# Modulation matmuls four in a row on one 1024-column tile, with loads two groups ahead, in a two-layer decoder step

## The chip, the cores and the metric

The kernel runs on one core of a Trainium2 chip, as one program. The time is the device time of one execution, in microseconds (us), the median of several runs. The engines are PE (TensorE, matmuls; its weight loads are listed apart as PEld), DVE (VectorE), ACT (ScalarE), POOL (GpSimd) and SP (SyncE), whose queue issues the transfers between HBM and the on-chip memory. Each engine, SP too, takes its instructions in one fixed order, and an instruction that waits holds up all that stand behind it on the same engine.

## The reference, cut to what matters

512 prompt tokens and 8 x 4 sample tokens (544 columns in all, in two halves of 272) go through two layers. Each layer has a mixer and a convolutional FFN, and both are wrapped in RMS norms with a shift, a scale and a gate per sequence (nine sequences: the prompt and eight samples), which come out of the conditioning vector c:

```python
c_act = jax.nn.silu(c)
for l in range(DEPTH):
    mod = (c_act @ w["ada_w"][l] + w["ada_b"][l])[:, None, :]      # (sequences, 1, 6 * 1024)
    sh1, sc1, g1, sh2, sc2, g2 = jnp.split(mod, 6, axis=-1)
    h = _rmsnorm(x, ng[0]) * (1 + sc1) + sh1
    y = mixer(h)                                                   # layer 0: _mixer_ab, layer 1: _mixer_cd
    x = x + g1 * _rmsnorm(y, ng[1])
    h = _rmsnorm(x, ng[2]) * (1 + sc2) + sh2
    y, f_new = _conv_ffn(h, f_prev, w["ffn_w_up"][l], ...)
    x = x + g2 * _rmsnorm(y, ng[3])
```

The matrix `ada_w` is 1024 x 6144 per layer in fp32, 50 MB in both, and is needed for nine rows only.

## The kernel before, in words

**The GEMMs.** The large products run in `gemm` and `mm` (lines 522 to 563). A fp32 weight block of 1024 x 128 comes in two raw tiles of 128 x 512 (256 KB each). `load_w` (504 to 512) issues the load on SP, lets ACT write a high part `whi` (line 510) and DVE or POOL the rest `wlo` (line 511). The input is kept likewise as `Hhi` and `Hlo`. Each of the eight 128-row pieces of a block then takes three products (lines 527, 529, 531) on two halves of 272 columns, 48 matmuls per block. The first blocks of a GEMM (its lead) and the last (its tail) are worked half by half. The raw tiles rotate through a ring of seven places with the tag `wraw` in the pool `wp`; `whi` and `wlo` have rings of eight. A tile takes the next place of its ring in the order in which the code asks for it, and may be written once the last reader of what was there is done.

**The modulation.** `ada(l, s)` (397 to 430) makes a third of one layer's modulation: 2048 columns, six calls in all. Per step k of eight it loads four tiles of 128 x 512 (line 403) and multiplies each with the 32 columns of `cact` (line 404), one in each of the four 32-column groups of PE, into one PSUM tile `psada`. After step 8 ACT copies `psada` to `adaev` (line 407, a tile of the norm pool), four PE transposes turn it (`psadat`, line 410), and DVE adds the bias and makes the scales cA and the gates cG (lines 411 to 429). The tiles come from the ring `wraw` in the start, later from a pool of six, then of four.

**The order.** `weave` (316) runs a GEMM block by block and a second generator beside it: after each block that takes one step, so the modulation of the next stage is spread over the GEMM of this one. `delay`, `pace` and `slow` (325 to 341) set how many steps per block. A scheduler then sets each engine's order from the whole program, so a matmul of the modulation stands where its load is expected, also in the middle of a block. The stages are: the start (modulation of layer 0's first third, X, the norm's `psn` sums, lines 440 to 449), mixer 0 with `w_abi` and `w_abo` from about 47 to 245 us, a junction (`postres` and `premod`, lines 461 to 502), FFN 0 with `w_up0` and `w_dn0` to about 660 us, mixer 1, FFN 1.

**Bias vectors.** `bias_vectors` (1188 to 1201), woven into FFN 0 ahead of layer 1's modulation, makes the attention bias in three steps. Each loads `ohp`, multiplies (`psrv`, line 1198), copies on ACT (line 1199) and stores to `rvd` in HBM through SP (line 1200). Its tiles come from the same pool as the modulation's.

Of the kernel before, what the change touches and what calls it, by code (L numbers as in the profile page):

```python
# [41 lines left out]
XRB = 6  # L42
# [225 lines left out]
def build(nc, tc, ctx, t):  # L268
# [120 lines left out]
    apool = []  # L389

    def ada_tile():
        if apool:
            ap, n = apool[-1]
            return ap.tile([P, CH, HT], F32, name="adaw", bufs=n).rearrange("p a n -> p (a n)")[:, 0:512]
        return wp.tile([P, 512], F32, name="adaw", tag="wraw", bufs=WRAW)

    def ada(l, s):
        ps = psum1("psada")
        for k in range(KB):
            for j in range(4):  # L400
                wt = ada_tile()
# [15 lines left out]

        def ng(i):
            oo = PAR["norm_g"][0] + (l * 4 + i) * KB
            return par[:, oo:oo + KB].unsqueeze(2).to_broadcast([P, KB, NMOD])  # L420

        mb = mods[l]
        if s == 0:
            V.scalar_tensor_tensor(cA[l][0], mb[:, 8:16, :], 1.0, ng(0), op0=ADD, op1=M)
        elif s == 1:
            V.tensor_tensor(cG[l][0], mb[:, 16:24, :], ng(1), op=M)
        else:
            V.scalar_tensor_tensor(cA[l][1], mb[:, 32:40, :], 1.0, ng(2), op0=ADD, op1=M)
# [93 lines left out]
    def mm(ps, wt, src, h0, h1):  # L522
        last = len(wt) - 1
        for i, (whi, wlo) in enumerate(wt):
# [93 lines left out]
    def ffn(l, nxt, side, pre):  # L618
# [55 lines left out]
        def body():  # L674
# [613 lines left out]
```

## Time and profile before

| | us |
|---|---|
| median of 3 runs | 1501.05 (1498.82 to 1502.52) |
| profiled execution, its own time | 1496.03 |
| its span, first to last instruction | 1494.3 |
| PE busy in the span | 1417.8 (95%) |
| modulation matmuls (line 404), busy | 102.6 |
| mean granted PE clock | 0.978 of full |

The profile is one execution; busy time counts each microsecond of an engine once. Matmuls overlap, so that a start-to-start distance tells more of their cost than a duration. A row of the timeline gives the start, the length up to the end of the last of the instructions that it groups, and in brackets the idle time before it and what ended that. An fp32 matmul leaves two records.

### The profile page before, as it was taken

To read this page: it belongs to the slowest core of one execution; us is meant where nothing else is said; L and a number is where in the kernel's file an instruction comes from. 1 tells how busy PE (TensorE), PEld (TensorE's weight loads), DVE (VectorE), ACT (ScalarE), POOL (GpSimd) and SP (SyncE) were. 2 spreads that over 40 slices of the span, in tenths; PEclk is the share of its full clock that TensorE was granted. 3 is DMA by queue.
4 is the path that set the end of the run, shared out by engine and by line. 5 is a ranking of instruction groups with operands and counts; after the bars stand their busy time and mean duration, and the time that the engine had idled before them with its cause. 6 is when DMAs were issued, how large, how long until landed. Compare 5 with 4: busy or idle time off the path is not lost.

```text
span 1494.3 us, 26853 instructions
## 1 busy us (share of the span) xinstructions
PE 1417.8 (95%) x10354; PEld 1271.0 (85%) x10354; DVE 882.1 (59%) x1788; ACT 618.8 (41%) x1145; POOL 170.6 (11%) x384
## 2 busy tenths in 40 slices
PE   6899997999999999999799999999699999999995
PEld 2578897988798798899699999678599999999995
DVE  1664427753165346446859979652886456456457
ACT  2322235743244234235652442643674444244244
POOL 0210014110011001001500000000521011011011
PEclk9799998999999999999999999999899999999998
DMA  7775633325445546544236245446122332332311
GB/s 264 242 253 187 201 106 100 103 98 180 160 155 194 161 139 212 165 158 186 89 113 197 94 141 178 135 146 239 57 85 69 103 93 71 104 91 65 113 51 61
DMA packets 112633, 207.72 MB, mean 139 GB/s; under 512 B 20884, under 2 KB 33684, under 8 KB 111992
## 3 DMA queue, kind: packets, MB, share of 16 engines
q1 hardware_dynamic: 112504, 206.00, 42.5%
q8 instruction: 81, 1.33, 0.4%
q14 instruction: 48, 0.39, 0.1%
HBM read 198.63 MB, written 34.39 MB: 156 GB/s over the span
## 4 chain that ended last, share of the span: by engine, by line
PE 88%; DVE 6%; DMA 2%; ACT 2%; issue 1%; SPq 0%; POOL 0%; POOLq 0%; DVEq 0%; ACTq 0%
PE psmm L527 23%; PE psmm L531 23%; PE psmm L529 23%; PE psada L404 6%; PE psn L442 2%; PE psmh L529 2%; PE psmh L527 2%; PE psmh L531 2%; PE pso L1013 1%; PE psl L979 1%; PE psl L981 1%; DVE X L492 1%; DVE Yf L491 1%; DVE Y L491 1%; DVE Hlo L481 1%
## 5 line engine op out<-in xcount | busy, mean ns | idle before, releaser
L510 ACT ACTIVATE whi<-wraw 128x512 fp32r<-128x512 f32 (+1 forms) x404 | 239.8, 600 | 511.4 <-PE psmm L529 411.6
L527 PE MATMUL psmm<-Hhi,whi 128*128 128x272 f32 x2028 | 435.9, 291 | 1.0 <-DVE extu L750 1.0
L531 PE MATMUL psmm<-Hhi,wlo 128*128 128x272 f32 x2028 | 431.4, 289 | 0.3 <-POOL wlo L511 0.3
L529 PE MATMUL psmm<-Hlo,whi 128*128 128x272 f32 x2028 | 430.0, 288 | 0.0
L511 DVE TENSOR_TENSOR wlo<-wraw,whi 128x512 fp32r<-128x512 f32 (+1 forms) x374 | 240.8, 649 | 303.4 <-ACT whi L510 288.3
L527 PEld LDWEIGHTS psmm<-Hhi,whi 128*128 128x128 f32 x2028 | 321.4, 189 | 24.3 <-issue 12.6
L529 PEld LDWEIGHTS psmm<-Hlo,whi 128*128 128x128 f32 x2028 | 322.5, 189 | 9.0 <-issue 9.0
L531 PEld LDWEIGHTS psmm<-Hhi,wlo 128*128 128x128 f32 x2028 | 321.5, 189 | 9.9 <-issue 9.2
L527 PE MATMUL psmm<-act_hi,whi 128*128 128x272 f32 x624 | 135.5, 290 | 0.0
L531 PE MATMUL psmm<-act_hi,wlo 128*128 128x272 f32 x624 | 135.3, 289 | 0.0
L529 PE MATMUL psmm<-act_lo,whi 128*128 128x272 f32 x624 | 132.7, 288 | 0.0
L578 DVE SCALAR_TENSOR_TENSOR fz<-fext,par,fz 128x560 f32<-128x560 f32 x88 | 70.5, 801 | 74.3 <-ACT fz L577 74.2
L404 PE MATMUL psada<-adaw,cact 128*32 128x512 f32 x384 | 102.6, 628 | 8.3 <-DMA adaw<-ada_w 8.3
L527 PEld LDWEIGHTS psmm<-act_hi,whi 128*128 128x128 f32 x624 | 99.6, 188 | 11.8 <-issue 8.4
L531 PEld LDWEIGHTS psmm<-act_hi,wlo 128*128 128x128 f32 x624 | 99.6, 188 | 7.6 <-issue 7.5
L529 PEld LDWEIGHTS psmm<-act_lo,whi 128*128 128x128 f32 x624 | 99.1, 188 | 0.8 <-issue 0.8
L577 ACT ACTIVATE fz<-fext,par 128x560 f32<-128x560 f32 x88 | 75.2, 855 | 34.5 <-DVE fext L647 34.5
L874 DVE SCALAR_TENSOR_TENSOR zd<-extd,par,zd 128x512 f32<-128x512 f32 x120 | 87.0, 746 | 0.7
L569 POOL COPY fso<-fext 128x2 f32<-128x2 f32 x88 | 23.1, 263 | 530.6 <-ACT fext L646 530.6
L579 DVE SCALAR_TENSOR_TENSOR fz<-fext,par,fz 128x560 f32<-128x560 f32 x88 | 70.5, 801 | 2.7
L646 ACT ACTIVATE fext<-psmm 128x512 f32<-128x512 f32 (+1 forms) x88 | 49.7, 564 | 51.1 <-PE psmm L531 51.1
L527 PE MATMUL psmh<-Hhi,whi 128*128 128x272 f32 x148 | 48.2, 326 | 16.1 <-ACT Hhi L479 14.5
(260 smaller groups left out, 1692.9 us busy)
## 6 DMA issues: line engine op xcount, KB each, us to landing
adaw<-ada_w SPq DMA_DIRECT2D x192, 256.0 KB, 3.6
wraw<-w_up SPq DMA_DIRECT2D x176, 256.0 KB, 3.0
wraw<-w_dn SPq DMA_DIRECT2D x64, 256.0 KB, 2.8
o_c<-cache SPq DMA_DIRECT2D x8, 2040.0 KB, 10.0
wraw<-w_cdi SPq DMA_DIRECT2D x52, 256.0 KB, 4.6
wraw<-w_abi SPq DMA_DIRECT2D x32, 256.0 KB, 4.5
o_c<-cache SPq DMA_DIRECT2D x8, 1016.0 KB, 7.1
kc<-kc SPq DMA_DIRECT2D x28, 256.0 KB, 3.7
```

The lines of the kernel that those rows point to most:

```text
L404: PE.matmul(ps[32 * j:32 * j + 32, :], cact[:, k, :], wt, start=(k == 0), stop=(k == KB - 1))
L442: PE.matmul(ps, ones, a, start=(i == 0), stop=(i == n - 1))
L510: A.activation(hi[:, :n], raw[:, :n], AF.Copy)
L511: eng.tensor_tensor(lo[:, :n], raw[:, :n], hi[:, :n], op=SUB)
L527: PE.matmul(ps[:, h, :HT], whi, xhi[:, h, :], start=(i == 0), stop=False)
L529: PE.matmul(ps[:, h, :HT], whi, xlo[:, h, :], start=False, stop=False)
L531: PE.matmul(ps[:, h, :HT], wlo, xhi[:, h, :], start=False, stop=(i == last))
L577: A.activation(z[:, :n], ext[:, 2:2 + n], AF.Identity, bias=b, scale=w[:, 2:3])
L578: V.scalar_tensor_tensor(z[:, :n], ext[:, 1:1 + n], w[:, 1:2], z[:, :n], op0=M, op1=ADD)
L579: V.scalar_tensor_tensor(z[:, :n], ext[:, 0:n], w[:, 0:1], z[:, :n], op0=M, op1=ADD)
L646: A.activation(fpr(ext, 2, h0, h1), cpr(ps, h0, h1), AF.Copy)
L874: V.scalar_tensor_tensor(cpr(z), ip, dw[:, i:i + 1], cpr(z), op0=M, op1=ADD)
```

## The change

`ada` takes a list of halves of the old calls. A step k of a half has four matmuls of 256 columns (line 420 of the changed code) that read one tile of 128 x 2 x 512, loaded by one transfer of 512 KB (line 409). Three such tiles rotate in a pool of their own, first the one of the start, later one of mixer 0 or of FFN 0. Loads are asked for two steps ahead of the matmuls. `tc.issue_after` holds each group of four behind the last matmul of the newest GEMM block, which `mm` notes in `newest`. As soon as step 8 of a half is asked for, `ada_out` does what follows it: `adaev`, now 128 x 256, comes from the weights' ring `wraw`; two matmuls with a selector `ssel` replace the four transposes and write only the 36 columns that are used; DVE does half of each sum. The tiles of `bias_vectors` (`bv`) come from the ring `wraw` too. In the start the statistics of both halves are made early (`xstat`), `xprep` and `first` of the second half move behind the first half of `w_abi`'s lead, and the normalised tiles `xr` come from the norm pool. The pacing is set anew for each stage.

```diff
-XRB = 6
+ADB = (3, 3)
...
+    ssel = cp.tile([P, 4, NMOD], F32, name="ssel")
+    apool = [st0]
+    newest = []
     def ada_tile():
-        if apool:
-            ap, n = apool[-1]
-            return ap.tile([P, CH, HT], F32, name="adaw", bufs=n).rearrange("p a n -> p (a n)")[:, 0:512]
-        return wp.tile([P, 512], F32, name="adaw", tag="wraw", bufs=WRAW)
-    def ada(l, s):
-        ps = psum1("psada")
-        for k in range(KB):
-            for j in range(4):
-                wt = ada_tile()
-                o = s * 2048 + j * 512
-                SY.dma_start(wt, t["ada_w"][l, k, :, o:o + 512])
-                PE.matmul(ps[32 * j:32 * j + 32, :], cact[:, k, :], wt, start=(k == 0), stop=(k == KB - 1))
-            yield
-        ev = np_.tile([P, 512], F32, name="adaev", tag="nsq", bufs=NSQ)
+        return apool[-1].tile([P, 2, 512], F32, name="adaw", bufs=ADB[len(apool) - 1])
+    def ada(halves, per, ahead):
+        todo = [(l, s, q, k) for l, s, q in halves for k in range(KB)]
+        tiles = []
+        def load():
+            if todo[len(tiles):]:
+                l, s, q, k = todo[len(tiles)]
+                tiles.append(ada_tile())
+                SY.dma_start(tiles[-1], t["ada_w"][l].rearrange("k p (s a q n) -> s q k p a n", s=3, a=2, q=2)[s, q, k])
+        for _ in range(ahead):
+            load()
+        for i, (l, s, q, k) in enumerate(todo):
+            load()
+            if k == 0:
+                ps = psum1("psada")[:, 0:256]
+            wt = tiles[i]
+            with tc.issue_after(newest[0]) if newest else nullcontext():
+                for j in range(4):
+                    PE.matmul(ps[32 * j:32 * j + 32, :], cact[:, k, :], wt[:, j // 2, 256 * (j % 2):256 * (j % 2) + 256],
+                              start=(k == 0), stop=(k == KB - 1))
+            if k == KB - 1:
+                ada_out(l, s, q, ps)
+            if i % per == per - 1:
+                yield
+    def ada_out(l, s, q, ps):
+        if q == 0 and l == 0 and s == 0:
+            V.tensor_copy(ssel, ident.rearrange("p (j n) -> p j n", j=4)[:, :, 0:NMOD])
+        ev = wp.tile([P, 256], F32, name="adaev", tag="wraw", bufs=WRAW)
         A.activation(ev, ps, AF.Copy)
-        pt = psum1("psadat")
-        for c in range(4):
-            PE.transpose(pt[:, c * P:(c + 1) * P], ev[:, c * P:(c + 1) * P], ident)
+        pt = psum1("psadat")[:, 0:8 * NMOD].rearrange("p (j c n) -> p j c n", j=4, c=2)
+        for c in range(2):
+            PE.matmul(pt[:, :, c, :], ev[:, c * P:c * P + P], ssel, start=True, stop=True)
+        mb = mods[l][:, s * 16:s * 16 + 16, :].rearrange("p (a q c) n -> q p a c n", a=2, q=2)[q]
         o = PAR["ada_b"][0] + l * 48 + s * 16
-        V.tensor_tensor(
-            mods[l][:, s * 16:s * 16 + 16, :].rearrange("p (j c) n -> p j c n", c=4),
-            pt.rearrange("p (c j n) -> p j c n", c=4, j=4)[:, :, :, 0:NMOD],
-            par[:, o:o + 16].rearrange("p (j c) -> p j c", c=4).unsqueeze(3).to_broadcast([P, 4, 4, NMOD]),
-            op=ADD)
+        pb = par[:, o:o + 16].rearrange("p (a q c) -> q p a c", a=2, q=2)[q]
+        V.tensor_tensor(mb, pt.rearrange("p (a b) c n -> p a (b c) n", a=2), pb.unsqueeze(3).to_broadcast([P, 2, 4, NMOD]), op=ADD)
         def ng(i):
-            oo = PAR["norm_g"][0] + (l * 4 + i) * KB
-            return par[:, oo:oo + KB].unsqueeze(2).to_broadcast([P, KB, NMOD])
-        mb = mods[l]
+            oo = PAR["norm_g"][0] + (l * 4 + i) * KB + 4 * q
+            return par[:, oo:oo + 4].unsqueeze(2).to_broadcast([P, 4, NMOD])
+        d = slice(4 * q, 4 * q + 4)
         if s == 0:
-            V.scalar_tensor_tensor(cA[l][0], mb[:, 8:16, :], 1.0, ng(0), op0=ADD, op1=M)
+            V.scalar_tensor_tensor(cA[l][0][:, d], mb[:, 1], 1.0, ng(0), op0=ADD, op1=M)
         elif s == 1:
-            V.tensor_tensor(cG[l][0], mb[:, 16:24, :], ng(1), op=M)
+            V.tensor_tensor(cG[l][0][:, d], mb[:, 0], ng(1), op=M)
         else:
-            V.scalar_tensor_tensor(cA[l][1], mb[:, 32:40, :], 1.0, ng(2), op0=ADD, op1=M)
-            V.tensor_tensor(cG[l][1], mb[:, 40:48, :], ng(3), op=M)
-        yield
+            V.scalar_tensor_tensor(cA[l][1][:, d], mb[:, 0], 1.0, ng(2), op0=ADD, op1=M)
+            V.tensor_tensor(cG[l][1][:, d], mb[:, 1], ng(3), op=M)
...
 def mm(ps, wt, src, h0, h1):
-                PE.matmul(ps[:, h, :HT], wlo, xhi[:, h, :], start=False, stop=(i == last))
+                x = PE.matmul(ps[:, h, :HT], wlo, xhi[:, h, :], start=False, stop=(i == last))
+        newest[:] = [x.ins]
...
-        weave(gemm(t["w_abi"], order, 0, KB, srcH, ev, lead=LEAD0, mids=(pre, None), loaded=loaded), side, drain=False)
+        weave(gemm(t["w_abi"], order, 0, KB, srcH, ev, lead=LEAD0, mids=(pre, None), loaded=loaded), sides[0])
...
-                   out_evac(Y, acc, cG[0][0], True, True), tail=TAIL, mids=(None, lambda: junction(0, Y, acc, nxt))), side)
+                   out_evac(Y, acc, cG[0][0], True, True), tail=TAIL, mids=(None, lambda: junction(0, Y, acc, nxt))), sides[1])
...
     def bias_vectors():
-        rel = ada_tile()[0:64, 0:12]
+        def raw():
+            return wp.tile([P, 512], F32, name="bv", tag="wraw", bufs=WRAW)
+        rel = raw()[0:64, 0:12]
         SY.dma_start(rel, t["rel"])
         for c in range(3):
-            oh, rv = ada_tile()[0:64, :], ada_tile()[0:12, :]
+            oh, rv = raw()[0:64, :], raw()[0:12, :]
             SY.dma_start(oh, t["ohp"][:, c * 512:(c + 1) * 512])
             ps = psum1("psrv")
             PE.matmul(ps[0:12, :], rel, oh, start=True, stop=True)
...
-    def xprep(h, c0, c1):
-        if c0 == 0:
-            XR[h] = rstd(squares(h), onesD)
-        r = XR[h].unsqueeze(1).to_broadcast([P, CH, HT])
-        for c in range(c0, c1, CH):
-            XR[h, c] = st0.tile([P, CH, HT], F32, name="xr", tag="adaw", bufs=XRB)
+    def xstat(h):
+        XR[h] = rstd(squares(h), onesD)
+    def xprep(h):
+        r = XR.pop(h).unsqueeze(1).to_broadcast([P, CH, HT])
+        for c in range(0, KB, CH):
+            XR[h, c] = np_.tile([P, CH, HT], F32, name="xr", tag="nsq", bufs=NSQ)
             V.tensor_tensor(XR[h, c], X[:, c:c + CH, h, :], r, op=M)
...
-    a = ada(0, 0)
+    a = ada([(0, 0, 0), (0, 0, 1)], 2, 2)
     steps(a, 3)
     for h in range(2):
         SY.dma_start(X[:, :, h, :], t["x"][:, :, h, :])
-    steps(a, 1)
     ao, io = PAR["a_w"][0], CST["flip"][0]
     SY.dma_start(par[:, :ao], t["par"][:, :ao])
     SY.dma_start(cst[:, :io], t["cst"][:, :io])
+    steps(a, 2)
+    xstat(0)
     steps(a, 1)
-    xprep(0, 0, KB)
-    steps(a, 1)
-    xprep(1, 0, CH * (XRB - 4))
+    xstat(1)
+    xprep(0)
     loaded = [load_block(t["w_abi"], ABI[i], 0, KB, (G, G)) for i in range(PRE)]
     for _ in a:
         pass
     first(0, 0, KB)
-    def second():
-        k = CH * (XRB - 4)
-        first(1, 0, k)
-        xprep(1, k, KB)
-        first(1, k, KB)
-    pre = mixer0((0, 1), chain(delay(1), pace(chain(ada(0, 1), ada(0, 2)), 7, 8)),
-                 second, loaded)
-    pre = ffn(0, (1, 0), chain(delay(8), bias_vectors(), slow(chain(ada(1, 0), ada(1, 1), ada(1, 2)), 2)), pre)
+    pre = mixer0((0, 1), (chain(delay(1), pace(ada([(0, 1, 0), (0, 1, 1), (0, 2, 0)], 1, 2), 3, 2)), ada([(0, 2, 1)], 1, 2)),
+                 lambda: (xprep(1), first(1, 0, KB)), loaded)
+    pre = ffn(0, (1, 0), chain(delay(8), bias_vectors(), pace(ada([(1, i, q) for i in range(3) for q in range(2)], 1, 2), 3, 4)), pre)
     pre = mixer1((1, 1), pre)
     ffn(1, None, caches(), pre)()
```

How the order moves, at three places. First PE in the GEMM `w_up0` of FFN 0, where layer 1's modulation is woven in. `psmm` is a GEMM block's sum, `psada` the modulation's; x2 counts equal instructions in a row. Before:

```order
L529 MATMUL psmm<-Hlo,whi 128x272 x2
L404 MATMUL psada<-adaw,cact 32x512 x2
L531 MATMUL psmm<-Hhi,wlo 128x272 x2
L527 MATMUL psmm<-Hhi,whi 128x272 x2
L529 MATMUL psmm<-Hlo,whi 128x272
L404 MATMUL psada<-adaw,cact 32x512
L529 MATMUL psmm<-Hlo,whi 128x272
L531 MATMUL psmm<-Hhi,wlo 128x272 x2
L527 MATMUL psmm<-Hhi,whi 128x272 x2
L529 MATMUL psmm<-Hlo,whi 128x272
L404 MATMUL psada<-adaw,cact 32x512
```

After, at the first group of that stage and, behind the dots, at the end of a half:

```order
L550 MATMUL psmm<-Hlo,whi 128x272 x2
L552 MATMUL psmm<-Hhi,wlo 128x272 x2
L420 MATMUL psada<-adaw,cact 32x256 x4
L548 MATMUL psmm<-Hhi,whi 128x272 x2
...
L552 MATMUL psmm<-act_hi,wlo 128x272 x2
L420 MATMUL psada<-adaw,cact 32x256 x4
L434 MATMUL psadat<-ssel,adaev 128x4x9 x2
L548 MATMUL psmm<-act_hi,whi 128x272 x2
```

The four matmuls of a step stand in a row now, between two products of a block. `psadat`, which needs the eviction by ACT of the sum just made, stands right behind the last four at the end of a half.

The second place is PE at the bias vectors, early in FFN 0. The names carry numbers here: `whi_2945` and `whi_2883` come from the loads `wraw_2944` and `wraw_2882`. Before, at the second of the three:

```order
L529 MATMUL psmm_2860<-Hlo_69,whi_2868 128x272 x2
L531 MATMUL psmm_2860<-Hhi_68,wlo_2869 128x272 x2
L1198 MATMUL psrv_2939<-adaw_2936,adaw_2851 12x512
L527 MATMUL psmm_2943<-Hhi_68,whi_2945 128x272 x2
L529 MATMUL psmm_2943<-Hlo_69,whi_2945 128x272 x2
```

After, at the first of the three:

```order
L550 MATMUL psmm_2802<-Hlo_69,whi_2810 128x272 x2
L552 MATMUL psmm_2802<-Hhi_68,wlo_2811 128x272 x2
L1222 MATMUL psrv_2877<-bv_2874,bv_2872 12x512
L548 MATMUL psmm_2881<-Hhi_68,whi_2883 128x272 x2
L550 MATMUL psmm_2881<-Hlo_69,whi_2883 128x272 x2
```

In both, `psrv` stands between two GEMM blocks. The third place tells which loads these blocks rest on. It is SP's queue around the store `rvd`, whose data ACT copies out of `psrv`. Before:

```order
L509 DMA wraw_3110<-w_up0 128x512
L509 DMA wraw_3116<-w_up0 128x512
L509 DMA wraw_3180<-w_up0 128x512
L509 DMA wraw_3186<-w_up0 128x512
L509 DMA wraw_3268<-w_up0 128x512
L1200 DMA rvd_94<-adaw_2854 12x512
L1196 DMA adaw_2936<-ohp 64x512
L509 DMA wraw_3274<-w_up0 128x512
```

The load `wraw_2944` stands ten rows ahead of this store. After:

```order
L530 DMA wraw_2803<-w_up0 128x512
L530 DMA wraw_2809<-w_up0 128x512
L1217 DMA bv_2872<-rel 64x12
L1220 DMA bv_2874<-ohp 64x512
L1231 DMA o_c1<-cache1 16x16256 x2
L1224 DMA rvd_98<-bv_2875 12x512
L530 DMA wraw_2882<-w_up0 128x512
L530 DMA wraw_2888<-w_up0 128x512
L1220 DMA bv_2957<-ohp 64x512
L1231 DMA o_c1<-cache1 16x16256
L1224 DMA rvd_98<-bv_2958 12x512
```

Before, the stores have six and more weight loads for later blocks ahead of them. After, the store `rvd` with the data of `psrv_2877` stands ahead of `wraw_2882` and `wraw_2888`, the two tiles of the block that follows `psrv_2877` on PE. Then SP at the first full block of `w_abi`, whose tiles are `wraw_696` and `wraw_702` after and `wraw_689` and `wraw_695` before. Before:

```order
L403 DMA adaw_416<-ada_w 128x512
L509 DMA wraw_434<-w_abi 128x512
L403 DMA adaw_419<-ada_w 128x512
L509 DMA wraw_689<-w_abi 128x512
L403 DMA adaw_422<-ada_w 128x512
L509 DMA wraw_695<-w_abi 128x512
L509 DMA wraw_788<-w_abi 128x512
```

After:

```order
L409 DMA adaw_572<-ada_w 128x2x512
L409 DMA adaw_623<-ada_w 128x2x512
L409 DMA adaw_676<-ada_w 128x2x512
L1231 DMA o_c0<-cache0 16x3968
L409 DMA adaw_682<-ada_w 128x2x512
L530 DMA wraw_696<-w_abi 128x512
L530 DMA wraw_702<-w_abi 128x512
```

Before, the two loads stand among the first modulation loads of the stage; after, behind ten of them, the last of which, `adaw_682`, takes the place of `adaw_572`, the last tile but one that PE reads ahead of that block.

## Rows read from the trace of the kernel before

**Rows 1.** The chain that ended last: share of the span by engine.
```profile
PE 88%; DVE 6%; DMA 2%; ACT 2%; issue 1%; SPq 0%; POOL 0%; POOLq 0%; DVEq 0%; ACTq 0%
```

**Rows 2.** Windows: busy us of each engine (x instructions), PE's granted clock, DMA share.
```profile
300.00:600.00 300.00, 300.00 (x2171) 258.35 (x2170) 142.03 (x267) 108.20 (x177) 22.91 (x89) 1.00 0.49 161
```

**Rows 3.** Windows of line 404's instructions alone: length, PE, PEld, clock, DMA share.
```profile
0.00:48.00 48.00, 23.26 (x64) 4.13 (x64) 0.93 0.82 278
48.00:1494.00 1446.00, 79.34 (x320) 11.06 (x320) 0.98 0.42 134
```

**Rows 4.** PE's timeline: start, length, instructions; visits of one and four, and psn.
```profile
71.86 0.29 PE L531 MATMUL psmm<-Hhi,wlo 128*128 128x272 f32 x1
72.08 1.05 PE L404 MATMUL psada<-adaw,cact 128*32 128x512 f32 x2
...
73.28 0.29 PE L529 MATMUL psmh<-Hlo,whi 128*128 128x272 f32 x1
...
404.17 0.41 PE L531 MATMUL psmm<-act_hi,wlo 128*128 128x272 f32 x2
404.51 1.06 PE L404 MATMUL psada<-adaw,cact 128*32 128x512 f32 x8
...
405.87 0.42 PE L529 MATMUL psmm<-Hlo,whi 128*128 128x272 f32 x2
...
28.77 2.10 PE L442 MATMUL psn<-nsq,onesD 128*128 128x272 f32 x8
```

**Rows 5.** PE's timeline around four transposes.
```profile
417.33 0.41 PE L531 MATMUL psmm<-Hhi,wlo 128*128 128x272 f32 x2
417.58 0.60 PE L410 MATMUL psadat<-cst,adaev 128*128 128x128 f32 x4
...
418.27 0.41 PE L529 MATMUL psmm<-Hlo,whi 128*128 128x272 f32 x2
```

**Rows 6.** PE's timeline after an idle time, and the window of that stretch.
```profile
252.02 1.28 PE L442 MATMUL psn<-yacc,onesD 128*128 128x272 f32 x2 [3.24 <-POOL yacc L606]
252.71 0.81 PE L529 MATMUL psmh<-Hlo,whi 128*128 128x272 f32 x1
...
258.03 0.28 PE L531 MATMUL psmm<-Hhi,wlo 128*128 128x272 f32 x1
...
252.70:258.00 5.30, 5.30 (x24) 5.18 (x23) 3.21 (x9) 1.99 (x5) 3.29 (x5) 0.50 0.16 49
```

**Rows 7.** Timeline of the start: last modulation matmuls, eviction, first GEMM matmul, a wait.
```profile
37.97 6.54 PE L404 MATMUL psada<-adaw,cact 128*32 128x512 f32 x16 [1.81 <-DMA adaw<-ada_w]
...
44.61 0.60 ACT L407 ACTIVATE adaev<-psada 128x512 f32<-128x512 f32 x1 [7.54 <-PE psada L404]
...
47.54 0.36 PE L527 MATMUL psmh<-Hhi,whi 128*128 128x272 f32 x1 [1.62 <-DVE Hhi L1238]
...
55.32 0.60 PE L529 MATMUL psmh<-Hlo,whi 128*128 128x272 f32 x1 [1.69 <-DVE Hlo L1239]
```

**Rows 8.** Waits of SP's queue, 48 to 660 us: total, times, longest.
```profile
SPq L1200 <- ACT adaw L1199: 26.5, 3, 16.3
```

**Rows 9.** Timeline of one bias vector: copy on ACT and store by SP.
```profile
326.10 0.59 ACT L1199 ACTIVATE adaw<-psrv 12x512 f32<-12x512 f32 x1 [0.51 <-PE psrv L1198]
...
326.72 0.32 SPq L1200 DMA_DIRECT2D rvd<-adaw  x1
```

**Rows 10.** DMA issues of the page: count, KB each, median us to landing.
```profile
wraw<-w_up SPq DMA_DIRECT2D x176, 256.0 KB, 3.0
...
wraw<-w_abi SPq DMA_DIRECT2D x32, 256.0 KB, 4.5
```

**Rows 11.** Landing of weight loads, 90 to 660 us, line of the tile's view.
```profile
DMA to landing us min/median/max: 2.0/4.3/7.6
```

**Rows 12.** Groups of the page: busy us, mean ns of one, idle before.
```profile
L510 ACT ACTIVATE whi<-wraw 128x512 fp32r<-128x512 f32 (+1 forms) x404 | 239.8, 600 | 511.4 <-PE psmm L529 411.6
...
L577 ACT ACTIVATE fz<-fext,par 128x560 f32<-128x560 f32 x88 | 75.2, 855 | 34.5 <-DVE fext L647 34.5
```

More of the change, by code (lines that the diff above doesn't have):

```diff
@@ L1 @@
 import numpy as np
-from contextlib import ExitStack
+from contextlib import ExitStack, nullcontext
 import concourse.bass as bass
@@ L290, in build @@
     cst = cp.tile([P, NCST], F32, name="cst")
+    er = ExitStack()
+    st0 = er.enter_context(pool("mix0r", side="right"))
     cact = cp.tile([P, KB, 32], F32, name="cact")
@@ L501, in junction, with load_w @@
             premod(nxt[0], nxt[1], h, lambda c, n: Y[:, c:c + n, h, :])
-    def load_w(ap, kc, eng):
+    def load_w(ap, eng):
         raw = wp.tile([P, 512], F32, name="wraw", tag="wraw", bufs=WRAW)
@@ L507, in load_w @@
         lo = wp.tile([P, 512], F32R, name="wlo", tag="wlo", bufs=WSLOTS)
-        n = kc * P
-        SY.dma_start(raw[:, :n], ap.rearrange("p k n -> p (k n)"))
+        n = ap.shape[1]
+        SY.dma_start(raw[:, :n], ap)
         A.activation(hi[:, :n], raw[:, :n], AF.Copy)
@@ L517, in load_block @@
             b = min(a + 4, k1)
-            hi, lo = load_w(w[n, :, a:b, :], b - a, eng[a // 4 % 2])
+            hi, lo = load_w(w[n, :, a:b, :].rearrange("p k n -> p (k n)"), eng[a // 4 % 2])
             out += [(hi[:, i * P:(i + 1) * P], lo[:, i * P:(i + 1) * P]) for i in range(b - a)]
@@ L630, in ffn @@
         if l == 0:
-            apool.append((fp, 4))
+            apool.append(fp)
         exts = [fp.tile([P, 562], F32, name=f"fext{i}") for i in range(FEXT)]
@@ L684, in body @@
             yield from down(ng - 1)
-            apool.clear()
+            del apool[1:]
         weave(body(), side)
@@ L692, in build, with mixer0 @@
     ABI = [12, 13, 14, 15] + [x for j in range(4) for x in (j, 8 + j, 4 + j)]
-    def mixer0(nxt, side, pre, loaded):
+    def mixer0(nxt, sides, pre, loaded):
         es = ExitStack()
@@ L699, in mixer0 @@
         acc = yacc()
-        apool.append((st0, XRB))
         ea = ExitStack()
@@ L784, in mixer0 @@
         er.close()
-        apool[-1] = (es.enter_context(pool("mix0w")), 4)
+        apool.append(es.enter_context(pool("mix0w")))
         ey = ExitStack()
@@ L788, in mixer0 @@
         weave(gemm(t["w_abo"], range(KB), 0, KB, lambda k: (yhi[:, k], ylo[:, k]),
-                   out_evac(Y, acc, cG[0][0], True, True), tail=TAIL, mids=(None, lambda: junction(0, Y, acc, nxt))), side)
+                   out_evac(Y, acc, cG[0][0], True, True), tail=TAIL, mids=(None, lambda: junction(0, Y, acc, nxt))), sides[1])
         es.close()
-        apool.clear()
+        del apool[1:]
         return lambda: (junction(1, Y, acc, nxt), ey.close())
@@ L1212, in build @@
     warm(cact[:, 0, 0:1])
-    er = ExitStack()
-    st0 = er.enter_context(pool("mix0r", side="right"))
     XR = {}
-    def xprep(h, c0, c1):
-        if c0 == 0:
-            XR[h] = rstd(squares(h), onesD)
-        r = XR[h].unsqueeze(1).to_broadcast([P, CH, HT])
-        for c in range(c0, c1, CH):
-            XR[h, c] = st0.tile([P, CH, HT], F32, name="xr", tag="adaw", bufs=XRB)
+    def xstat(h):
[4 more added lines that the diff above has]
+            XR[h, c] = np_.tile([P, CH, HT], F32, name="xr", tag="nsq", bufs=NSQ)
             V.tensor_tensor(XR[h, c], X[:, c:c + CH, h, :], r, op=M)
```

1 line of the change is left out of this document (removed).

## The prediction, made before the changed kernel was run

> **What bounds the kernel now.** I read the chain of waits first: PE holds 88% of the chain that ended last [rows 1]. Then the stage that the change touches: between 300 and 600 us PE is busy for all of 300 us at full clock [rows 2]. So wherever PE has no gap, each PE microsecond taken out is a microsecond gained, and each wait that appears on PE is a microsecond lost. The third reading is what the modulation costs there. Its matmuls were busy 102.60 us in all, 23.26 of them in the start, before the GEMMs run [rows 3]; the other 79.3 us stand between GEMM matmuls. A busy time is not a price, because matmuls overlap, so I took the price from the starts of the neighbours. GEMM matmuls start 0.125 us apart. Around a visit of one modulation matmul (two records) they start at 71.86 and, two later, at 73.28: 1.42 us where 0.25 is usual, so the visit costs 1.17. Around a visit of four (eight records) they start at 404.17 (two), and the second pair after that at 405.87: 1.70 where 0.50 is usual, so 1.20 [rows 4]. One matmul and four cost the same, since the four run side by side in their 32-column groups. The price is per visit, not per matmul.
>
> **The change part by part.**
> *Visits.* Counted in PE's order behind the start, before has 75 visits: 40 groups of four, of which many are torn into single matmuls and pairs. 75 x 1.06 us busy is 79.5, which agrees with the 79.3 above. After has 73 visits: 80 groups of half the width, 66 alone and seven times two together. So the number hardly falls; what can fall is the length of one. The 512 columns of a visit are streamed for part of the 1.18 us, the rest is fixed. The split has no row. The nearest is psn, also fp32: four matmuls of 272 columns last 2.10 us [rows 4], 0.525 each with their end, thus about 0.43 to 0.5 for 256 columns. A half-width visit then costs 1.18 less this: 0.69 to 0.75. I take 0.75. The bounds are 0.59 (half, nothing fixed) and 1.18 (nothing streamed). Two groups together have the columns of one old visit: 1.18. Sum: 75 x 1.18 = 88.5 goes, 66 x 0.75 + 7 x 1.18 = 57.8 comes, **-30.7**.
>
> [...] Our rows, one matmul as dear as four, agree with a fixed part but do not size it. If it were all of the visit, this is rival B below.
>
> *Transposes.* Before, four transposes cost 0.44 us: starts 417.33 and 418.27, 0.94 where 0.50 is usual [rows 5]. Five sets behind the start, 2.2 us. After has ten behind the start, two matmuls each, and in its order they stand right behind the last group. PE must wait for the eviction on ACT that lies between: 128x512 takes 0.59 to 0.60 us [rows 7, 9], half the width by estimate 0.4, so 0.83 per set: 8.3. **+6**; bounds +3 (0.5 each) and +10.
>
> *Start.* The last eight modulation matmuls run one by one as their loads land, 6.54 us; then eviction at 44.61, transposes, and the first GEMM matmul at 47.54; and PE waits 1.69 us for Hlo at 55.32 [rows 7]. After works in groups of four, and half of the modulation, with its Hhi and Hlo, is ready a good 10 us earlier. Some 3 us of the 6.5, 2 of the tail and 1.7 of the wait can go: **-7**. Its load ring holds 1.5 MB in place of seven slots of 256 KB, so it may also be starved; bounds -10 and 0.
>
> *Late weight loads.* This is the term that decides. Two new users, the eviction tile `adaev` and the bias tiles `bv`, take places in the weights' ring of seven. SP's order is one queue: a weight load behind an instruction that waits waits as well. Before, no weight block that PE needs next stands so. After has these:
> - Bias vectors, three times. In after's SP order the store `rvd` stands ahead of the two loads of the very block that follows `psrv` on PE. The store needs the copy on ACT, which needs `psrv`. Before, this copy takes 0.59 us and the store 0.32 [rows 9]; SP waited 26.5 us on it in three times [rows 8], without harm, because loads for blocks further on were ahead. Now the chain copy 0.59, store 0.32, landing 3.0 (w_up) [rows 10], cast 0.60 [rows 12] and some 0.3 of hand-overs lies bare: 4.8 each, 14.4.
> - The first full w_abi block: its loads are behind five modulation loads, the last of which waits for the last group but one ahead of the block. Two issues of 0.4 us by estimate, landing 3.7 (between w_up's 3.0 and w_abi's 4.5 [rows 10]), cast 0.6, hand-overs 0.3, less the 1.6 that PE spends on the last visit and the transposes: 3.8. A second w_abi block alike: 3.6. One in w_abo's tail: 1.3.
> - The first w_down block, whose load needs a slot that an eviction held: 4.2.
> - The junction to the first FFN: before, w_up loads are far ahead, and PE does the first half's GEMM while the second half's norm is made. After, `psn` stands ahead of that GEMM, and the loads behind the fso load, which waits for the mixer's last matmul. Of the 12 us of work some 3 come too late to fill the gap: 3 (bounds 0 and 5).
> Sum **+30.3**. With a landing of 2.0, the shortest [rows 11], it is 23; with 4.5, w_abi's median, some 41.
>
> [...]
>
> *Clock.* [...] Seven of the new waits last over 3 us: six above, and one in the next paragraph. 7 x 2.6 = **+18.2**. Bounds: 0 (no fall) and 21 (eight).
>
> *Casts behind evictions.* In after's ACT order weight casts stand behind `adaev` at six places where PE is close behind. In five of these the cast comes 0.8 to 2.35 us late: 6.3. In the sixth ACT's order is adaev, fz, silu, cast, with two steps on DVE between: 0.4, 0.86, then the steps and silu by estimate 0.8 each, 0.6 [rows 12]: 4.3, and hand-overs of 0.1 to 0.2 each: 4.9. **+11.2**, bounds 4 and 16.
>
> Hidden, at nothing: the 512 KB loads themselves (SP issues 80 in place of 160 in the weave, and the bytes are the same), DVE's small mods, twice as many at half size. They run beside PE; what it costs if that cover goes is in the terms above. Mixer 1 and the second FFN keep their order.
>
> **Sum:** -30.7 + 6 - 7 + 30.3 + 18.2 + 11.2 = **+28.0**. The profiled execution took 1496.0 us, so such a one of after takes 1524; the median of the runs shown is 1501.05, 5 above, so 1529 beside it.
>
> **The rivals.**
> *A, faster: the late loads are covered.* It is one mechanism: SP reaches the loads early enough, or the ring's slack of two blocks holds, so that the last three terms, 59.7 as priced, come to less than 31.7, where the sum is zero. For it: SP's waits of before harmed nobody [rows 8], and landing can be 2.0. Against: in the bias chain no slack exists, as the chain begins with the matmul ahead of the block. With the bias chain only (14.4 and three clock falls, 7.8) the sum is -9.5: 1491.5.
> *B, slower: a visit does not shrink with its columns.* 73 x 1.18 = 86.1, a gain of 2.4 only: +56.3, 1557. For it: one and four matmuls cost alike. Against: psn's length shows that fp32 columns take time.
> *C: the clock does not fall after these waits.* +9.8, 1511. For it: the waits are scattered in full-speed work. Against: rows 7.
>
> **How the numbers follow.** The forecast (all terms as priced, give or take 15) has 0.60, A 0.14, B 0.08, C 0.18. The time is the forecast's, 1529. The range reaches down to 1499, below C's and over some of A's, and up to 1550, which takes in landings of 4.5 us; left out are B and most of A. About 0.3% either way, 4.5 us, is what a measurement of this kernel can tell from no change: faster is A less its upper edge, 0.12; same is the rest of A and the lower edge of C, 0.08; slower 0.80.
>
> **What would show it.** In the profile of the changed kernel: half-width visits, neighbours' starts 0.75 us further apart (1.18 would be B); three waits of PE of 4 to 5 us for casts or loads right behind `psrv`; PE idle in front of the first full w_abi block and of w_down; the granted clock below 1 behind them; the first GEMM matmul at 41 to 43 us. PE without waits between 90 and 660 us would make A right and the forecast wrong by 40 us.

## The result, and the profile after

| | before | after |
|---|---|---|
| median, us | 1501.18 | 1538.18 (1537.44 to 1540.36, 4 runs) |
| ratio to before | | 1.0251 (95% interval 1.0233 to 1.0268) |
| profiled execution, its own time | 1496.03 | 1537.44 |

The change makes the kernel slower by 37.0 us in the median. Between the two profiled executions the distance is 41.4, because the profiled execution of before lies 5 under its median and that of after does not. The range held the time; the forecast of 1529 was 9 too low in the median, and its sum of +28.0 was 13.4 too low beside the 41.4.

The page of the changed kernel: the span, PE's busy time, PE's granted clock in 40 slices, and the engines of the chain that ended last.

```profile
span 1535.7 us, 27491 instructions
...
PE 1411.4 (92%) x10762; PEld 1297.3 (84%) x10762; DVE 888.5 (58%) x1803; ACT 622.6 (41%) x1151; POOL 163.5 (11%) x384
...
PEclk9899998989999999999899999999799999999998
...
PE 83%; DVE 7%; DMA 5%; ACT 3%; issue 1%; SPq 1%; POOL 0%; POOLq 0%; DVEq 0%; ACTq 0%
```

PE is busy 6.4 us less than before, in a span that is 41 longer. What was added is waiting, and the chain says so: PE's share falls from 88% [rows 1] to 83%, and transfers come in. The waits of PE between 48 and 680 us (engine, line, what it waited for: total, times, longest):

```profile
PE psmm L548 <- ACT whi L531: 35.6, 10, 5.5
PE psadat L434 <- ACT adaev L431: 4.1, 8, 0.6
PE psn L463 <- ACT nsq L479: 3.8, 1, 3.8
PE psmm L552 <- DVE wlo L532: 3.6, 5, 1.1
```

Before, the rows of PE in this stretch are full where the GEMMs run [rows 2]. Now ten waits for a weight cast, `whi` on ACT, hold 35.6 us. I compared the two traces matmul by matmul: the n-th GEMM matmul of after against the n-th of before gives the distance at each place. After stands 1.9 us ahead at the first GEMM matmul, 9.6 ahead at the 96th, 7.2 ahead at 104 us (the 288th), 4.5 behind at 228 (1056th), 6.8 behind at 277 (1248th), 30.4 behind at 351 (1632nd), 14.4 behind at 420 (2112th), 27.8 behind at the beginning of FFN 0's tail (4128th), and 37.4 behind at mixer 1's first matmul (4320th). So single places take time away in jumps, and it comes back in quiet stretches. The largest of these gains, 16 us between 351 and 420 us, is mostly a matter of place: before has 19 visits in that stretch of matmuls, after nine.

The price of a visit. PE's timeline of after around a visit of one group and of two (start, length, instruction):

```profile
103.24 0.41 PE L552 MATMUL psmm<-Hhi,wlo 128*128 128x272 f32 x2
103.57 0.64 PE L420 MATMUL psada<-adaw,cact 128*32 128x256 f32 x8
...
104.50 0.41 PE L550 MATMUL psmm<-Hlo,whi 128*128 128x272 f32 x2
...
110.01 0.41 PE L552 MATMUL psmm<-Hhi,wlo 128*128 128x272 f32 x2
110.35 1.07 PE L420 MATMUL psada<-adaw,cact 128*32 128x256 f32 x16
...
111.71 0.41 PE L550 MATMUL psmm<-Hlo,whi 128*128 128x272 f32 x2
```

From 103.24 (two matmuls) to the second pair behind the visit are 1.26 us where 0.50 is usual: 0.76. With two groups, from 110.01 to 111.71: 1.70, so 1.20. Before, [rows 4], a visit of any number cost 1.17 to 1.20. The median of 55 undisturbed visits is 0.77.

The dearest places are the three bias vectors; here is the first of them. Timeline of after, all engines:

```profile
294.96 1.02 PE L1222 MATMUL psrv<-bv 64*12 64x512 f32 x2
...
296.03 0.59 ACT L1223 ACTIVATE bv<-psrv 12x512 f32<-12x512 f32 x1 [0.30 <-PE psrv L1222]
...
296.64 0.38 SPq L1224 DMA_DIRECT2D rvd<-bv  x1
...
297.12 0.84 SPq L530 DMA_DIRECT2D wraw<-w_up  x2
...
300.00 0.63 ACT L531 ACTIVATE whi<-wraw 128x512 fp32r<-128x512 f32 x1 [2.64 <-DMA wraw<-w_up]
...
300.68 0.50 PEld L548 LDWEIGHTS psmm<-Hhi,whi 128*128 128x128 f32 x2 [5.62 <-ACT whi L531]
```

Here the whole chain of the prediction can be read from top to bottom. `psrv` begins on PE at 294.96. ACT copies it at 296.03. SP issues the store at 296.64 and only then the two weight loads, from 297.12. ACT casts the first at 300.00, and PE goes on at 300.68, after 4.69 us idle. SP's own waits between 290 and 298.1 us have this row:

```profile
SPq L1224 <- ACT bv L1223: 26.4, 1, 26.4
```

The queue stood 26.4 us in front of this store. The two weight loads behind it (line 530) have no row there: they waited for nothing of their own, so their places in the ring were free, and the queue's order alone held them. Before, the copy and the store took the same 0.59 and 0.32 us [rows 9], and PE did not wait, since the block's weights had been loaded long before.

The same shape stands at the first full block of `w_abi`: SP issues the block's loads at 74.95, straight behind the modulation load that waited for a visit; they are cast at 79.53 and PE goes on at 80.22, after 4.16 us:

```profile
74.48 0.37 SPq L409 DMA_DIRECT2D adaw<-ada_w  x1
...
74.95 0.89 SPq L530 DMA_DIRECT2D wraw<-w_abi  x2
...
79.53 1.28 ACT L531 ACTIVATE whi<-wraw 128x512 fp32r<-128x512 f32 x2 [3.56 <-DMA wraw<-w_abi]
...
80.22 0.60 PE L548 MATMUL psmm<-Hhi,whi 128*128 128x272 f32 x1 [4.16 <-ACT whi L531]
```

Behind such waits PE runs at a granted clock of 0.50 for a while; here behind the one that ended at 300.68. Windows of after (length, then busy us of PE, PEld, DVE, ACT, POOL with instructions, granted clock, DMA share, GB/s):

```profile
300.68:304.90 4.22, 4.22 (x18) 4.22 (x19) 1.36 (x2) 0.63 (x1) 0.00 (x0) 0.50 0.65 245
```

These are 18 matmuls in 4.22 us, where 0.125 each would be 2.25: the granted clock is 0.50, as in [rows 6].

### The profile page after: what moved, and what is told of

It reads as the page before. It is cut to its first block, busy times and chain, and to the rows that moved or that the text cites. A ratio compares the mean times of both kernels' runs of the same rounds, so it can differ in the third digit from the quotient of the medians.

```text
span 1535.7 us, 27491 instructions
## 1 busy us (share of the span) xinstructions
PE 1411.4 (92%) x10762; PEld 1297.3 (84%) x10762; DVE 888.5 (58%) x1803; ACT 622.6 (41%) x1151; POOL 163.5 (11%) x384
## 2 busy tenths in 40 slices
DMA packets 111097, 207.74 MB, mean 135 GB/s; under 512 B 19348, under 2 KB 32148, under 8 KB 110456
## 3 DMA queue, kind: packets, MB, share of 16 engines
q1 hardware_dynamic: 110968, 205.99, 41.4%
## 4 chain that ended last, share of the span: by engine, by line
PE 83%; DVE 7%; DMA 5%; ACT 3%; issue 1%; SPq 1%; POOL 0%; POOLq 0%; DVEq 0%; ACTq 0%
PE psmm L548 23%; PE psmm L552 22%; PE psmm L550 22%; PE psada L420 3%; PE psn L463 2%; PE psmh L548 2%; PE psmh L552 2%; PE psmh L550 2%; PE pso L1034 1%; DMA X<-x 1%; DMA wraw<-w_abi 1%; PE psl L1000 1%; PE psl L1002 1%; DVE Hlo L502 1%; DVE X L513 1%
## 5 line engine op out<-in xcount | busy, mean ns | idle before, releaser
L548 PEld LDWEIGHTS psmm<-Hhi,whi 128*128 128x128 f32 x2028 | 326.2, 191 | 48.4 <-ACT whi L531 33.4
L552 PEld LDWEIGHTS psmm<-Hhi,wlo 128*128 128x128 f32 x2028 | 327.2, 191 | 7.6 <-DVE wlo L532 3.4
L550 PEld LDWEIGHTS psmm<-Hlo,whi 128*128 128x128 f32 x2028 | 326.2, 191 | 2.8 <-issue 2.6
L420 PE MATMUL psada<-adaw,cact 128*32 128x256 f32 x768 | 64.5, 417 | 12.5 <-DMA adaw<-ada_w 12.5
L463 PE MATMUL psn<-nsq,onesD 128*128 128x272 f32 x128 | 44.6, 498 | 19.9 <-ACT nsq L479 19.9
```

The costliest lines, as they stand in the source:

```text
L420: PE.matmul(ps[32 * j:32 * j + 32, :], cact[:, k, :], wt[:, j // 2, 256 * (j % 2):256 * (j % 2) + 256], start=(k == 0), stop=(k == KB - 1))
L463: PE.matmul(ps, ones, a, start=(i == 0), stop=(i == n - 1))
L548: PE.matmul(ps[:, h, :HT], whi, xhi[:, h, :], start=(i == 0), stop=False)
L550: PE.matmul(ps[:, h, :HT], whi, xlo[:, h, :], start=False, stop=False)
L552: x = PE.matmul(ps[:, h, :HT], wlo, xhi[:, h, :], start=False, stop=(i == last))
```

## Experiments

Eight kernels ran. Their ratios are to the kernel before, each with its 95% interval. The theory is that `adaev` and the bias tiles, by taking places in the weights' ring, make the scheduler put weight loads behind instructions on SP that wait. The main rival is that the larger transfers make loads late whatever ring they use.

**e1: bias tiles out of the weights' ring.**

```diff
-            return wp.tile([P, 512], F32, name="bv", tag="wraw", bufs=WRAW)
+            return np_.tile([P, CH, HT], F32, name="bv", tag="nsq", bufs=NSQ).rearrange("p a n -> p (a n)")[:, 0:512]
```

> The changed kernel with one edit: the bias-vector tiles come from the norm pool's ring instead of the weights' ring. Theory (ring places): the three waits of PE behind psrv (4.69, 5.53 and 5.40 us in the changed kernel's trace, 15.6 together) go, and with them half-clock stretches of 6.8, 6.8 and 3.4 us, of which half is lost, 8.5: 24 us less, about 1514 us. Rival (busier transfers: 512 KB loads and the cache copies keep the queue late whatever ring is used): three waits of over 4 us stay and the time is 1532 to 1538.

Measured: 1515.98 us, ratio 1.0103 (1.0076 to 1.013), 22.2 less than the changed kernel. PE's waits of e1 between 270 and 330 us, where three waits held 15.6:

```profile
PE psmm L552 <- POOL wlo L532: 1.0, 1, 1.0
PE psmm L548 <- ACT whi L531: 0.4, 1, 0.4
```

All three are gone, and the time is the theory's to 2 us. In part that is luck: in the traces 21.3 us are gained between the 1344th and the 1728th GEMM matmul, where the bias vectors stand and 24 were expected, and another 5.7 between the 3600th and the 4032nd, since the wait of 4.18 us at `w_dn`, which the theory left standing, is gone too; 3.5 are lost ahead of the 1344th and 4.3 from mixer 1 on. The transfers are the same as in the changed kernel (207.74 MB in 111097 packets in both); the order in which SP issues them differs. The rival falls for this part.

**e2: the eviction tile out of the weights' ring.**

```diff
-        ev = wp.tile([P, 256], F32, name="adaev", tag="wraw", bufs=WRAW)
+        ev = np_.tile([P, 256], F32, name="adaev", tag="nsq", bufs=NSQ)
```

> The changed kernel with one edit: the eviction tile adaev comes from the norm pool's ring instead of the weights' ring. Theory: the four waits for weights at the w_abi, w_abo and w_dn blocks (4.16, 3.63, 3.46, 4.18 us) go with about 10 us of half clock behind them, and since in this kernel's order only 2 of the 12 transposes stand right behind the last group (10 in the changed kernel), some 4 us of waits for the eviction go too: about 30 us less, 1508 us. The three waits behind psrv stay. Rival (busier transfers): the waits in front of these blocks stay, 1532 to 1538.

Measured: 1506.37 us, ratio 1.0040 (1.0023 to 1.0056), 31.8 less. The waits for weights at the `w_abi`, `w_abo` and `w_dn` blocks are gone; the one at `w_dn` goes in e1 as well, so either edit is enough for it. In 270 to 330 us those behind `psrv` stay, three of them, as expected; two new ones, of 1.41 and 3.07 us, stand at `w_up` blocks at 409 and 651 us, the second in the other row here:

```profile
PE psmm L548 <- ACT whi L531: 14.8, 3, 5.1
...
650.72 0.53 PE L548 MATMUL psmm<-Hhi,whi 128*128 128x272 f32 x2 [3.07 <-ACT whi L531]
```

**e3: both.** The two edits together.

> Both edits of the two runs before: neither adaev nor the bias tiles take places in the weights' ring. Theory: the gains add, 24 + 30, about 1484 us, which is below the kernel before (1501). What then stays of the cost is the tail of FFN 0 (11 us in the changed kernel). Rival (busier transfers): 1530 or more. Rival (the gains overlap, because a load that is late once gives the queue time to run ahead): 1495 to 1505.

Measured: 1482.26 us, ratio 0.9883 (0.9861 to 0.9905). The gains add: 22.2 + 31.8 = 54.0, and 55.9 were measured. Neither the busier transfers nor an overlap of the two is needed to explain these times. So nearly the same visits and the same loads are 1.2% faster than the kernel before, once two small tiles rotate in another ring. In the profiles e3 is 23.6 us ahead of before at mixer 1's first matmul and 13.3 at the end: the rest is given back in code that no edit touches. What is left of PE's waits between 48 and 680 us is led by:

```profile
PE psadat L434 <- ACT adaev L431: 4.8, 1, 4.8
PE psmh L548 <- DVE Y L630: 2.2, 1, 2.2
PE psmh L548 <- DVE act_hi L604: 1.8, 1, 1.8
```

The 4.8 us are one wait, for the last eviction of layer 0's modulation in `w_abo`'s tail: in e3's trace ACT makes four steps of the junction (1.70 us from 222.70) ahead of that eviction at 224.31, and they in turn wait for DVE.

**e4: both, and the modulation of layer 1 earlier in FFN 0.**

```diff
-... pace(ada([(1, i, q) for i in range(3) for q in range(2)], 1, 2), 3, 4) ...
+... pace(ada([(1, i, q) for i in range(3) for q in range(2)], 1, 2), 1, 1) ...
```

> As the run before, and layer 1's modulation is paced at one step per GEMM block in FFN 0 instead of three steps in four blocks, so that its last group stands some 300 PE rows ahead of where it stood, in front of FFN 0's tail. Theory (modulation in the tail holds accumulator banks that the tail's blocks need as filler while the last activation is made): the tail's 11 us go, about 1473 us, and the waits for act_hi (2.68 us) and for the last adaev (0.81) are not there. Rival (the tail's wait is that of the last activation and stands whatever the modulation does): 1484, as the run before.

Measured: 1484.72 us, ratio 0.9900 (0.9875 to 0.9926): no gain over e3. This expectation missed, and the trace shows where. From the 4032nd to the 4320th GEMM matmul, FFN 0's tail and the 96 matmuls ahead of it, e4 gains 7.5 us on e3, and the wait for `act_hi` is 0.3 instead of 1.8 us:

```profile
PE psmm L548 <- ACT whi L531: 1.8, 1, 1.8
...
PE psmh L548 <- DVE act_hi L604: 0.3, 1, 0.3
```

It is 2.4 ahead at the 96th matmul, in the start, which is the same code in both. From the 96th to the 4032nd matmul it loses 5.0, among them a new wait of 1.8 us for a weight cast at 521.67, whose cause stays open; and in mixer 1 and behind it loses 8.2 more, in code that neither kernel changes. That last stretch takes 765 to 783 us in the profiles of e3 to e8, an unexplained spread as large as the gains in question. The place of the theory was right, and the tail's gain was given back elsewhere.

The traces show what the tail lacks with modulation in it. The last activation is not later: it is complete 5.1 us behind the tail's first matmul in the changed kernel, 5.4 in e3, 6.1 in e4 and 5.8 before. But PE's order has 18, 27, 45 and 43 GEMM matmuls there, in that sequence of kernels, ahead of the first one that needs it, and the wait for it is 2.68, 1.81, 0.33 and 0.32 us. Why the order comes out so (the accumulator banks that `psada` and `psadat` hold, or something else in the scheduler) was not tried and stays open.

**e5: two steps together in FFN 0.** On top of e3.

```diff
-... pace(ada([(1, i, q) for i in range(3) for q in range(2)], 1, 2), 3, 4) ...
+... pace(ada([(1, i, q) for i in range(3) for q in range(2)], 2, 2), 3, 8) ...
```

> As the run with both tiles in the norm pool (1482), and in FFN 0 two steps of the modulation go together, at the same mean pace, so that two groups of four can share a visit. In PE's order 25 visits then hold eight matmuls and 28 hold four, where the run before had 7 and 64. Theory (a visit of PE costs 0.34 us fixed and 0.43 per half-width group, from 0.77 for one group and 1.20 for two in the changed kernel's trace): 6 us less, 1476. Rival (with three tiles the second group of a pair comes too late, and PE waits for its load): 1482 or more, with waits of PE for adaw in FFN 0.

Measured: 1478.38 us, ratio 0.9856 (0.9832 to 0.9880); 3.9 less than e3 where 6 were expected. No wait of PE for `adaw` exists between 60 and 660 us, so the rival falls:

```profile
PE psadat L434 <- ACT adaev L431: 5.0, 2, 4.8
PE psmh L548 <- DVE Y L630: 2.2, 1, 2.2
PE psn L463 <- POOL yacc L628: 1.3, 1, 1.3
PE psmm L550 <- DVE Hlo L1262: 1.1, 1, 1.1
PE psmm L552 <- DVE wlo L532: 0.9, 1, 0.9
```

By PE's order and the prices above its visits cost 53 us where e3's cost 59. In the trace e5 gains 3.4 us on e3 between the 192nd and the 4032nd GEMM matmul; 0.9 of the missing rest is the wait for `wlo` in the list, the other part was not found.

**e6: no hold.** On top of e3.

```diff
-            with tc.issue_after(newest[0]) if newest else nullcontext():
+            with nullcontext():
```

> As the run with both tiles in the norm pool (1482), without the hold behind the newest GEMM block. Theory (the four matmuls stand together because they read one tile that lands at once; the hold adds nothing): PE's order has 72 visits in place of 73, and the time is 1482 within 4. Rival (the hold is what keeps the groups together and PE from waiting for their loads): waits for adaw on PE and 1490 or more.

Measured: 1482.14 us, ratio 0.9876 (0.9854 to 0.9898): the same as e3. PE has no wait for `adaw` between 60 and 660 us, so the rival falls. The groups stay together without the hold; that this is because they read one tile that lands at once fits, but was not tried with separate tiles. One visit even holds three groups. PE's timeline of e6:

```profile
57.60 0.29 PE L552 MATMUL psmm<-Hhi,wlo 128*128 128x272 f32 x1
57.82 1.50 PE L420 MATMUL psada<-adaw,cact 128*32 128x256 f32 x24
...
59.48 0.29 PE L550 MATMUL psmm<-Hlo,whi 128*128 128x272 f32 x1
```

From 57.60 to the second matmul behind the visit are 1.88 us where 0.25 is usual: 1.63. One group is 0.77, two are 1.20, three 1.63.

**e7: layer 0's last half earlier.** On top of e3.

```diff
-... ada([(0, 2, 1)], 1, 2) ...
+... pace(ada([(0, 2, 1)], 1, 2), 2, 1) ...
```

> As the run with both tiles in the norm pool (1482), and the last half of layer 0's modulation is woven into w_abo at two steps per block instead of one, so that its eviction no longer falls into w_abo's tail, where PE waited 4.80 us for adaev in that run's trace. Theory: this wait and some 2 to 3 us of half clock behind it go, about 1475. Rival (the junction behind is bound by the norm's chain, so that PE only waits there instead): 1480 to 1484.

Measured: 1481.12 us, ratio 0.9866 (0.9838 to 0.9893): 1.1 under e3, inside the rival's bounds. The wait of 4.80 us is gone, and at FFN 0's first matmul e7 has gained 5.5 us on e3 since the 960th. But PE then waits for the norm's chain in the junction:

```profile
225.17 1.28 PE L463 MATMUL psn<-nsq,onesD 128*128 128x272 f32 x3 [2.88 <-ACT nsq L479]
...
244.13 1.27 PE L463 MATMUL psn<-yacc,onesD 128*128 128x272 f32 x2 [3.25 <-POOL yacc L628]
```

and 3.1 us of the gain are given back by the 1728th matmul, behind the bias vectors; by the 2112th e7 is 0.8 behind e3, so that nothing of it is left. The rival was right: PE had been waiting in one place for what binds in the next.

**e8: pairs, early half and an earlier end in FFN 0.** e5 and e7 together, paced at 5, 12 instead of 3, 8.

> The pairs of the first and the early gate of the third of these runs together, with FFN 0's modulation paced at 12 blocks for 10 steps, so that it ends about 190 PE rows ahead of FFN 0's tail. Theory (the gains add: 6 for the visits, 7 for the gate, 5 for the tail's wait): about 1465. Rival (the tail's gain is given back in the weave and behind, as in the run with the pace alone): 1470 to 1473. Below 1482 in any case if visits and gate each give half of what is expected.

Measured: 1476.58 us, ratio 0.9841 (0.9814 to 0.9869), the fastest that was run, 1.6% under the kernel before. It is 5.7 under e3 but cannot be told from e5. The gains do not add, as in e4: between the 4032nd and the 4320th matmul e8 gains 4.4 us on e3, but between the 1152nd and the 4032nd GEMM matmul it has lost 9.6, of which 4.4 are three waits for weight casts (0.74, 1.18 and 2.44 us) that e3 does not have, and some 4 are the early half's gain, given back in the junction as in e7.

## Why the prediction was right, and where its size was off

The working of the forecast, term by term, in us, beside what the trace of after has:

| term | forecast | trace |
|---|---|---|
| visits | -30.7 | -29.3 (66 x 0.77 + 7 x 1.20 = 59.2 for 88.5) |
| transposes | +6 | +7.8 |
| start | -7 | -5.7 |
| late weight loads | +30.3 | +33.4 |
| clock | +18.2 | +16.4 |
| casts behind evictions | +11.2 | +7.8 |
| FFN 0's tail | 0 | +9.6, of which 2.6 are in the first two rows too |
| mixer 1 and behind | 0 | +4.0 |
| sum | +28.0 | +41.4 with the 2.6 taken once, as the spans show |

The tail's 9.6 us hold two visits (1.5) and one set of transposes (1.1) that the first two rows count already, so 7.0 are its own. The six terms that the forecast priced come to +30.4 where it had +28.0; single ones are off by up to 3.4, and these errors mostly cancel. The other 11.0 have no term in it. The median misses by less, 9.2 instead of 13.4, because the forecast added 5 us to come from the profiled execution to the median, and after's profiled execution lies 0.7 under its median: that part is luck.

*Visits.* The estimate of 0.75 from psn's length was right: 0.77. The three sizes of a visit give 0.43 for a group and 0.34 for the rest. Rival B is refuted by these rows: a visit shrinks with its columns. What the fixed 0.34 us consists of no run shows.

*Transposes.* One set of after: the last group ends, PE waits 0.50 us for the eviction, and the two matmuls run:

```profile
391.61 0.41 PE L552 MATMUL psmm<-act_hi,wlo 128*128 128x272 f32 x2
...
391.95 0.64 PE L420 MATMUL psada<-adaw,cact 128*32 128x256 f32 x8
...
393.09 0.64 PE L434 MATMUL psadat<-ssel,adaev 128*128 128x36 f32 x4 [0.50 <-ACT adaev L431]
...
393.97 0.41 PE L550 MATMUL psmm<-act_lo,whi 128*128 128x272 f32 x2
```

From 391.61 to 393.97 are 2.36 us where 0.50 is usual. Less 0.77 for the visit that is 1.08 per set, where 0.83 was taken: the way from PE to ACT ahead of the eviction, 0.5 of the 1.08, had been put at less. Nine sets are 9.7, a tenth costs 0.3; 2.2 goes.

*Start.* The 9.6 us of lead at the 96th matmul hold 3.9 of cheaper visits. The first matmul came 1.9 earlier, not 5; the rest is that Hlo's wait [rows 7] is gone and that the granted clock is back at 1.00 at about 49 us, which before happened at 60.

*Late loads.* Each place that was named has its wait: 4.16 (forecast 3.8) and 3.63 (3.6) at `w_abi`, 3.46 (1.3) at `w_abo`, 4.69, 5.53 and 5.40 (4.8 each) behind `psrv`, 4.18 (4.2) at `w_dn`. At the junction the distance grows by 2.3 (3). e1 and e2 show the cause: each tile taken out of the ring takes its waits away. At `w_dn` the size is right and the reason is not. The forecast had that load wait for a place that an eviction held; in the trace the block's first load, issued at 663.57, waits for nothing of its own, and ahead of it on SP stands a modulation load that waited for a visit (SP's waits, 660 to 664.1 us):

```profile
SPq L409 <- PE psada L420: 9.3, 1, 9.3
```

In e1 two loads of `w_dn` stand ahead of that modulation load, and PE does not wait.

*Clock.* It fell to 0.50 in nine places, not seven, and stayed there for 3.4 or 6.8 us each time, but a part of that lies in the wait itself, while PE idles. Half of what is left comes to 16.4, or 1.8 each, where the forecast had 2.6 from one stretch of before: 22 matmuls in 5.32 us where 2.75 is usual, at a granted clock of 0.50 [rows 6]. Rival C is refuted. (Against it the forecast names rows 7; the rows with the clock are [rows 6].)

*Casts.* The large one was 3.33 and 0.88 us (4.9), the others 0.5 to 1.1.

*FFN 0's tail*, a term that the sum does not have, is its largest miss. What the forecast puts at nothing or unchanged are the 512 KB loads, DVE's small work, mixer 1 and the second FFN; this tail it does not name. In the kernel before, the last modulation visit stands 433 GEMM matmuls ahead of the tail's first one (at 637.13 and 692.52 us). In after the modulation runs into the tail, and PE waits for the activation and for the last eviction at a granted clock of 0.50; rows of after, and the window:

```profile
725.51 0.60 PE L548 MATMUL psmh<-act_hi,whi 128*128 128x272 f32 x1 [2.68 <-DVE act_hi L604]
...
730.66 1.07 PE L434 MATMUL psadat<-ssel,adaev 128*128 128x36 f32 x4 [0.81 <-ACT adaev L431]
...
724.80:738.50 13.70, 11.59 (x52) 8.85 (x53) 7.39 (x22) 7.34 (x15) 0.00 (x0) 0.50 0.54 173
```

The tail of before, its one wait and its window, at a granted clock of 1.00:

```profile
698.39 0.39 PE L527 MATMUL psmh<-act_hi,whi 128*128 128x272 f32 x1 [0.32 <-DVE act_hi L582]
...
690.00:705.00 15.00, 14.68 (x118) 14.46 (x116) 9.19 (x24) 7.05 (x15) 0.38 (x2) 1.00 0.75 281
```

e4 bears out the place: with the modulation ended earlier this stretch is 7.5 us shorter than in e3. With 7.0 us of its own the tail is the largest part of the 13.4 by which the sum was low. The 4.0 behind it are mostly two jumps, of 1.5 us at 754 to 758 and 1.9 at 1071 us of before's trace, in code that the change leaves alone. At the first, the granted clock of after falls to 0.50 for 3.4 us behind a wait of 3.00 us, and that of before, behind 1.68 us in the same place, stays at 1.00. Nothing was run on them, and with a spread of 765 to 783 us for this stretch in e3 to e8, beside 764.7 and 768.7 in before and after, the 4.0 cannot be put down to the change.

Rival A is refuted as told, but e3 is that rival made true: the late loads, with their clock and casts, are gone. The first three terms alone would make 1469; e3 has 1482, with FFN 0's tail (5.5 us to the 4224th matmul) and the wait of 4.8 us left.

## What to carry to other kernels

A small tile that takes a place in a ring of load buffers can be dear: here two of them cost 22.2 and 31.8 us, because weight loads then stood behind instructions that waited, 26.4 and 9.3 us in the two rows of SP's waits above, on a queue that issued in order. Read the issuing queue's order for each block's loads and ask what the instruction ahead of them waits for; where it is the work just ahead of that block, the whole chain of copy, store, landing and cast is bare. Four matmuls that shared one tile stayed together by themselves here; no hold was needed for it (e6).

## What the runs showed of the hardware

A visit of four fp32 matmuls in 32-column groups cost 0.34 us fixed and 0.43 us per 256 columns (0.77, 1.20, 1.63 for one, two and three groups). With 512 columns one matmul cost as much as four side by side, 1.17 and 1.20 us [rows 4].

At each of eight waits of 3.3 to 5.5 us in otherwise full PE work the granted clock of after fell to 0.50, for 3.4 or 6.8 us, and so it did at three shorter ones close together (0.5, 0.8 and 1.1 us between 595 and 599 us); at single waits of 0.5 to 0.6 us (at 169, 394 and 529 us) it stayed at 1.00. The length of a wait alone does not decide it: behind the 3.07 us of e2 at 650.72 the clock stayed at 1.00, as this window of e2 shows:

```profile
650.70:656.00 5.30, 5.28 (x40) 5.11 (x41) 3.99 (x6) 3.77 (x6) 0.00 (x0) 1.00 1.03 367
```

In windows of 0.5 us over the whole of before and of after the granted clock has two levels, 0.50 and 1.00; only the windows in which it changes lie between them.
